# Low parts of an attention phase moved from GpSimd to VectorE, and three of fifteen prepared weight slabs parted later

## Chip, cores and metric

One core of one Trainium2 chip runs the whole program. The metric is the device time of one execution in microseconds (us); the median of several runs counts.

## What is computed

Two transformer blocks follow each other, on 1024 tokens of width 1024, in float32. The first has a convolution and retention mixer and an MLP; the second has sparse attention (DSA, 8 heads that share one key), latent attention (MLA, 8 heads), a gated merge and an MLP. The change touches the projection and the attention of the second block, and a preparation that runs inside the first. The reference of the second block, shortened:

```python
h = rmsnorm(x, attn_norm_g)
z = h @ w_in          # a_q, a_k, a_v, i_q, i_k, i_w, c_q, c_kv, k_r, g
y_a = dsa_sparse_attention(a_q, a_k, a_v, i_q, i_k, i_w, positions, rel_bias)   # top 256 keys of a query
q_nope, q_rope = split(rmsnorm(c_q) @ w_uq)
k_nope, v_b = split(rmsnorm(c_kv) @ w_ukv)
y_b = mla_attention(q_nope, rope(q_rope), k_nope, rope(k_r), v_b)
gates = sigmoid(g + b_gate)
x = x + (gates[0] * (y_a @ w_branch_a) + gates[1] * (y_b @ w_branch_b)) @ w_out
```

## The kernel before

**Products.** Each float32 product is three TensorE products of rounded parts: high by high, high by low, low by high (`mm3`, line 528). A high part (`wh` for weights, halves of `u` or `t` for data) is a rounding copy, on ScalarE; a low part (`wl`, and others) is the difference of the number and its high part, a subtraction. `unit` (line 534) is the product of a 1024 x 128 piece of a weight with 512 tokens: 24 matmuls of 128x512. In it the background work gets a tick four times, once for every six matmuls (`Background`, line 195).

**Weights.** `Stream` (line 344) brings the weights in the order of use: the sync engine (SP) loads 512 KB into a ring of three (`wr`), ScalarE makes the high part, and the engine in `lo_engine` makes the low one. An entry made by `parted` needs none of this: GpSimd's DMA queue fetches both parts, ready, from the scratch `slabd` in DRAM.

**Preparation.** `part_slabs` (line 2017) fills `slabd` during the first block, 15 slabs in two halves each, in two lanes of the background. A lane loads half a slab into one of two `t4` buffers by SP, yields for some ticks, then queues the high part on ScalarE, the low part on VectorE and the write to `slabd` on GpSimd's DMA queue, each by a tick of its own. ScalarE takes its instructions in order, so the one of the slab stands ahead of all that is queued behind it, whether its load has landed or not.

**Projection of the second block.** `z_phase` (line 2323) multiplies `h` by all columns of `w_in`. The bit search for the top 256 keys (`topk` lane) runs beside it on VectorE and ScalarE. Its last ten units, for the columns AK (key and value of DSA) and AQ to AQ+3P (queries of DSA), come as five weights for the first 512 tokens and the same five again for the second, each fetched twice from `slabd`. Two halves of `w_uq` and then `w_ukv`, which follow in the stream, are split as usual.

**Attention.** `attention` (line 2425) writes its order by a planner, `Plan` (line 273). Each `step` has an engine, a cost, a rank and needs; the planner keeps a clock of its own for each engine and takes the step that starts first, so the costs fix the order in which instructions stand on each engine. Heads 0 to 7 are MLA, 8 to 15 DSA. A head has a front (logits into PSUM, row maximum and biases on VectorE, exponentials on ScalarE) and a back (transposes, products with values). The low parts are steps of "Pool", which is GpSimd: of the rope rows of the key (`mla_begin`, line 2670) and of the queries (`rope_rows`, 2780), of the DSA queries and key (`dsa_inputs`, 2833, `dsa_begin`, 2861), of the attention outputs (`y_done`, 2603, `yb_part`, 2918) and of the first three branch weights (`branch_weights`, 2467); so are the additions that end `q_rope` (2689). GpSimd also issues most of attention's DMAs.

Of the kernel before, what the change touches and what calls it, by code (L numbers as in the profile page):

```python
# [11 lines left out]
F32 = mybir.dt.float32  # L12
# [7 lines left out]
P = 128  # L20
# [468 lines left out]
class Model:  # L489
# [922 lines left out]
    def plan_mlp(self, w1, w2):  # L1412
# [3 lines left out]
        for q in range(16):  # L1416
            c = 2 * q * P
            s.add(D, [(lambda raw: raw.rearrange("p (k m) -> p k m", k=8), w1[:, :, c:c + P])])
        for q in self.QUADS:
            self.plan_quad(w1[:, :, 2 * q * P:2 * q * P + P], w1[:, :, 2 * q * P + P:2 * q * P + 2 * P])  # L1420
        x = {"t": [None, None], "b": [None, None]}
# [65 lines left out]

    def plan_quad(self, wa, wb):

# [478 lines left out]
    def plan2(self):  # L1968
# [19 lines left out]
        lat, rest = [CQ, CQ + P, CKV], [AK, AQ, AQ + P, AQ + 2 * P, AQ + 3 * P]  # L1988
        self.slabs = gates[:2] + lat + gates[2:] + rest
        for cs in (gates[:2], lat, lat, gates[2:], rest, rest):  # L1990
            for c in cs:
                s.parted(self.slabd[:, self.slabs.index(c)], D)
        self.slabs = [w[:, c:c + P].rearrange("(k p) m -> p k m", p=P) for c in self.slabs]
        wq = a["w_uq_2"]
# [22 lines left out]
    def part_slabs(self, e):  # L2017
# [4 lines left out]
        for i, h in halves[e::2]:  # L2022
# [5 lines left out]
            nc.sync.dma_start(raw.rearrange("p (k m) -> p k m", k=4), self.slabs[i][:, 4 * h:4 * h + 4])  # L2028
            yield 2
            yield (raw,)  # L2030
# [292 lines left out]
    def z_phase(self, hs, f, acc, G2):  # L2323
# [65 lines left out]
        for m in range(NZ - 3, 16):  # L2389
# [5 lines left out]
            if m == NZ - 2:  # L2395
                latent_products()
        for H in range(2):
            for kind, m in (("akv", 0), ("aq", 0), ("aq", 1), ("aq", 2), ("aq", 3)):
                w = ws.next()
                p = self.ps()  # L2400
                self.unit(p, w, hs[H])
                self.z_evac(kind, m, H, p)
        bg.flush()
# [21 lines left out]
    def attention(self):  # L2425
# [32 lines left out]
        ws = self.ws  # L2458
        ws.lo_engine = self.nc.gpsimd
        self.branch_weights(starts[15])  # L2460
# [6 lines left out]
    def branch_weights(self, t):  # L2467

        ws, step = self.ws, self.plan.step
        for i in range(3):  # L2470
            a = step("ACT", 0.95, t + i, lambda i=i: ws.split_ahead(ws.used + i + 1), [self.room])
            step("Pool", 2.4, t + i, lambda i=i: ws.parts[ws.used + i][2](), [a])

# [129 lines left out]
    def y_done(self, t, n, x):  # L2603
# [13 lines left out]
        def low(engine):  # L2617
            engine.tensor_sub(self.ya[1][:, s], x["ys"], self.ya[0][:, s].bitcast(F32))
        a = step("ACT", 0.95, t, high, needs + [self.room])
        if n < 15:  # L2620
            step("Pool", 2.4, t, lambda: low(nc.gpsimd), [a], frees=("t4",))
        else:
            step("DVE", 1.2, t, lambda: low(nc.vector), [a], frees=("t4",))
# [46 lines left out]
    def mla_begin(self):  # L2670
# [10 lines left out]
        for i in range(3):  # L2681
            kh, kl = self.slot(i)[2:4]
            a = self.plan.step("ACT", 0.95, -20 + i, lambda kh=kh: nc.scalar.activation(kh[64:96], kr, AF.Copy))
            self.kr_steps.append(self.plan.step(
                "Pool", 2.4, -20 + i, lambda kh=kh, kl=kl: nc.gpsimd.tensor_sub(kl[64:96], kr, kh[64:96].bitcast(F32)),
                [a]))
        self.qr_steps = {g: [self.q_rope(g, H) for H in range(2)] for g in range(2)}

    def q_rope(self, g, H):
# [19 lines left out]
        def main():  # L2709
# [6 lines left out]
        b = step("DVE", 0.61, rank, main, [b], frees=("ps",))  # L2716
        return step("Pool", 1.3, rank, lambda: nc.gpsimd.tensor_add(dst[:, c], dst[:, c], x["t"]), [a, b],
                    frees=("t2",))
# [61 lines left out]
    def rope_rows(self, t, h, done):  # L2780
# [11 lines left out]
        def low():  # L2792
            qh, ql = self.slot(h)[0:2]
            nc.gpsimd.tensor_sub(ql[64:96], x["raw"][64:96], qh[64:96].bitcast(F32))
# [3 lines left out]
        return step("Pool", 2.4, t + 2, low, [b], frees=("t4",))  # L2798

# [33 lines left out]
    def dsa_inputs(self, h):  # L2833
# [13 lines left out]
        def low():  # L2847
            nc.gpsimd.tensor_sub(self.aqs[64:128, s], x["raw"][0:64], self.aqs[0:64, s].bitcast(F32))

# [11 lines left out]
    def dsa_begin(self):  # L2861
# [56 lines left out]
    def yb_part(self, t, m, H):  # L2918
# [239 lines left out]
    def run(self):  # L3158
# [44 lines left out]
```

## Time and profile before

| | us |
|---|---|
| median of 3 runs (lowest, highest) | 2674.82 (2673.29, 2676.94) |
| the profiled execution, its own time | 2677.41 |
| its span, first to last instruction | 2675.6 |
| TensorE busy | 2588.6 (97%) |
| VectorE busy | 1895.2 (71%) |
| ScalarE busy | 1334.5 (50%) |
| GpSimd busy | 366.4 (14%) |

The profile names engines PE (TensorE), DVE (VectorE), ACT (ScalarE), POOL (GpSimd) and SP (the sync engine, which only issues DMAs). A row's operation is written as output<-inputs with the tiles' names: `ps` and `pd` are PSUM, the others SBUF. All operations go through one helper and so stand at one line, L183; they are told apart by tiles and shapes. "[17.77 <-DMA t<-in_w_in]" says that the engine stood idle for 17.77 us before the instruction, and that what ended the wait was a DMA. Block 1 ends shortly after 1200 us of the span, the second block's projection (the z phase) then runs to about 1506 us and attention from there to about 1850 us.

### The profile page before, as it was taken

Reading aid. Unit: us, or ns where it says so; the run is one execution under the profiler, and the core shown is the slowest. Engines: PE = TensorE matmul, PEld = TensorE weight load, DVE = VectorE, ACT = ScalarE, POOL = GpSimd, SP = SyncE. Lnnn points to the kernel's source line nnn. Section 1 sums busy time; section 2 is a strip of 40 time slices with the busy share of each in tenths; the row PEclk is TensorE's granted clock in tenths of the full one; section 3 lists DMA queues with packets and bytes.
Section 4 is the critical chain, followed back from the end, with each engine's and each line's share of the span. In section 5 each row is a group of like instructions: output and inputs, shape, how many; then the busy total and the mean of one; then the engine's idle time right before and its main releaser. Section 6 shows DMA issues by size and latency. Waiting matters only on the chain.

```text
span 2675.6 us, 33677 instructions
## 1 busy us (share of the span) xinstructions
PE 2588.6 (97%) x12052; PEld 2079.3 (78%) x12052; DVE 1895.2 (71%) x3239; ACT 1334.5 (50%) x2208; POOL 366.4 (14%) x393
## 2 busy tenths in 40 slices
PE   4999999999999999999999999999999999999998
PEld 4777777777888878777878778777887888887886
DVE  6684576887665466877889878887557566646668
ACT  4562114565444343445676477885135554443334
POOL 5141111100000021000211411420000000002111
PEclk8999999999999999999999999999999999999999
DMA  6536638655445597645545501444455564459784
GB/s 207 186 106 217 192 116 272 220 185 152 147 138 197 188 268 212 190 116 170 138 150 169 185 15 40 145 149 136 149 171 160 185 224 142 154 186 268 189 252 146
DMA packets 371735, 456.98 MB, mean 171 GB/s; under 512 B 34014, under 2 KB 262285, under 8 KB 371053
## 3 DMA queue, kind: packets, MB, share of 16 engines
q1 hardware_dynamic: 332096, 311.07, 37.2%
q0 software_dynamic: 39136, 143.60, 18.8%
q8 instruction: 95, 1.56, 0.2%
q14 instruction: 76, 0.61, 0.1%
q10 hardware_dynamic: 332, 0.14, 0.0%
HBM read 361.70 MB, written 96.18 MB: 171 GB/s over the span
## 4 chain that ended last, share of the span: by engine, by line
PE 73%; DVE 10%; issue 6%; DMA 5%; ACT 4%; POOL 1%; SPq 0%; POOLq 0%; ACTq 0%; DVEq 0%
PE ps L183 50%; PE pd L183 22%; DVE u L183 4%; DVE t L183 3%; ACT u L183 2%; DMA t<-in_w_in 2%; ACT t L183 1%; DVE wl L183 1%; DVE tiny L183 1%; POOL u L183 1%; DMA slabd<-t 1%; DVE topk L183 1%; DMA u<-opd 1%; ACT wh L183 1%; DMA t<-aqd 0%
## 5 line engine op out<-in xcount | busy, mean ns | idle before, releaser
L183 PE MATMUL ps<-u,wh 128*128 128x512 f32 x3696 | 1173.3, 398 | 6.7 <-ACT u L183 4.2
L183 PEld LDWEIGHTS ps<-u,wh 128*128 128x128 f32 x3696 | 690.0, 188 | 177.0 <-ACT u L183 5.7
L183 PE MATMUL ps<-u,wl 128*128 128x512 f32 x1848 | 731.9, 396 | 0.6 <-DVE wl L183 0.6
L183 PE MATMUL pd<-u,wh 128*128 128x512 f32 x1472 | 480.3, 407 | 2.5 <-ACT u L183 1.6
L183 PEld LDWEIGHTS ps<-u,wl 128*128 128x128 f32 x1848 | 347.5, 188 | 86.4 <-DVE wl L183 1.3
L183 DVE TENSOR_TENSOR wl<-wr,wh 128x1024 fp32r<-128x1024 f32 (+3 forms) x213 | 229.9, 1080 | 162.5 <-ACT wh L183 156.0
L183 PEld LDWEIGHTS pd<-u,wh 128*128 128x128 f32 x1472 | 274.1, 190 | 70.9 <-issue 5.7
L183 PE MATMUL pd<-u,wl 128*128 128x512 f32 x736 | 292.4, 397 | 0.0
L183 ACT ACTIVATE wh<-wr 128x1024 fp32r<-128x1024 f32 (+3 forms) x225 | 207.2, 921 | 168.3 <-PE pd L183 78.9
L183 ACT ACTIVATE t<-ps 128x512 f32<-128x512 f32 (+7 forms) x347 | 176.6, 523 | 177.0 <-PE ps L183 164.1
L183 DVE TENSOR_TENSOR t<-ps,t 128x384 fp32r<-128x384 f32 (+3 forms) x354 | 192.5, 563 | 90.6 <-PE ps L183 59.7
L183 ACT ACTIVATE t<-t 128x512 f32<-128x512 f32 (+2 forms) x261 | 162.8, 626 | 168.9 <-DVE t L183 90.5
L183 DVE TENSOR_TENSOR u<-u 128x1024 fp32r<-128x1024 f32 (+3 forms) x154 | 154.1, 1002 | 68.1 <-ACT u L183 62.6
L183 ACT ACTIVATE u<-t 128x512 fp32r<-128x512 f32 (+4 forms) x158 | 127.5, 815 | 136.7 <-DVE t L183 110.8
L183 ACT ACTIVATE wh<-u 128x1024 fp32r<-128x1024 f32 x96 | 101.3, 1055 | 182.8 <-PE ps L183 116.8
L183 DVE TENSOR_TENSOR wl<-u,wh 128x1024 fp32r<-128x1024 f32 x96 | 117.3, 1222 | 88.0 <-ACT wh L183 87.9
L183 PE MATMUL ps<-wh,u 128*128 128x512 f32 (+1 forms) x576 | 173.7, 383 | 0.6 <-DVE u L183 0.6
L183 POOL DMA_DIRECT2D u<-opd x64 | 55.2, 1027 | 862.8 <-DMA u<-opd 758.2
L183 PEld LDWEIGHTS pd<-u,wl 128*128 128x128 f32 x736 | 139.2, 189 | 34.0
L183 PE MATMUL pd<-wh,u 128*128 128x512 f32 x512 | 162.0, 396 | 0.0
L183 ACT ACTIVATE u<-u 128x1024 fp32r<-128x1024 f32 (+8 forms) x111 | 97.6, 889 | 126.1 <-issue 57.1
L183 ACT ACTIVATE u<-ps 128x512 f32<-128x512 f32 (+2 forms) x171 | 95.9, 575 | 115.2 <-PE ps L183 109.2
(191 smaller groups left out, 3507.6 us busy)
## 6 DMA issues: line engine op xcount, KB each, us to landing
wr<-in_w_fc SPq DMA_DIRECT2D x64, 512.0 KB, 4.5
opd<-t SPq DMA_DIRECT2D x128, 256.0 KB, 3.7
u<-opd POOLq DMA_DIRECT2D x64, 512.0 KB, 10.5
wr<-in_w_ff SPq DMA_DIRECT2D x64, 512.0 KB, 4.5
wr<-in_w_in SPq DMA_DIRECT2D x60, 512.0 KB, 3.9
t<-opd SPq DMA_DIRECT2D x48, 512.0 KB, 4.8
u<-in_w_ada POOLq DMA_DIRECT2D x32, 512.0 KB, 4.7
wr<-in_w_out SPq DMA_DIRECT2D x32, 512.0 KB, 3.9
```

What stands on the lines that cost most here:

```text
L183: return fn(*args, **kw)
```

## The change

1. `slabd` has 12 slabs instead of 15. AK, AQ and AQ+P are no longer prepared in block 1; their entries in block 2 are loaded and split as usual. AQ+2P and AQ+3P still come from `slabd`.
2. The last ten units of the z phase become five weights, each used at once for both halves of the tokens, into a pair of PSUM banks. There are as many matmuls as before.
3. A preparation lane yields 4 ticks instead of 2 between a slab's load and its high part on ScalarE.
4. Low parts of the weights fetched after that point, among them the two of `w_uq`, are made by VectorE instead of GpSimd.
5. In attention all steps of "Pool" become steps of "DVE", at lower costs, and the planner writes its order anew. GpSimd is left with DMA issues.
6. `plan_quad` counts its alternating half slots from the first of its entries, which keeps the alternation as it was.

```diff
@@ plan_mlp, plan_quad
+        first = len(s.entries)
-            self.plan_quad(w1[...], w1[...])
+            self.plan_quad(first, w1[...], w1[...])
...
+        n -= first_n
         s.entry(first, load, after, half=n % 2)
@@ plan2
-        self.slabs = gates[:2] + lat + gates[2:] + rest
-        for cs in (gates[:2], lat, lat, gates[2:], rest, rest):
+        self.slabs = gates[:2] + lat + gates[2:] + rest[3:]
+        for cs in (gates[:2], lat, lat, gates[2:]):
             for c in cs:
                 s.parted(self.slabd[:, self.slabs.index(c)], D)
+        for c in rest:
+            if c in self.slabs:
+                s.parted(self.slabd[:, self.slabs.index(c)], D)
+            else:
+                s.cols(w, c)
@@ part_slabs
-            yield 2
+            yield 4
@@ z_phase
-        for H in range(2):
-            for kind, m in (("akv", 0), ("aq", 0), ("aq", 1), ("aq", 2), ("aq", 3)):
-                w = ws.next()
-                p = self.ps()
-                self.unit(p, w, hs[H])
-                self.z_evac(kind, m, H, p)
+        ws.lo_engine = nc.vector
+        for kind, m in (("akv", 0), ("aq", 0), ("aq", 1), ("aq", 2), ("aq", 3)):
+            w = ws.next()
+            p = self.pd()
+            self.unit(p[:, 0], w, hs[0])
+            self.unit(p[:, 1], w, hs[1])
+            for H in range(2):
+                self.z_evac(kind, m, H, p[:, H])
@@ attention
-        ws.lo_engine = self.nc.gpsimd
@@ branch_weights; the same edit in y_done, mla_begin, rope_rows, dsa_inputs, dsa_begin
-            step("Pool", 2.4, t + i, lambda i=i: ws.parts[ws.used + i][2](), [a])
+            step("DVE", 1.14, t + i, lambda i=i: ws.parts[ws.used + i][2](), [a])
@@ q_rope; the same edit in yb_part
-        return step("Pool", 1.3, rank, lambda: nc.gpsimd.tensor_add(dst[:, c], dst[:, c], x["t"]), [a, b],
+        return step("DVE", 0.6, rank, lambda: nc.vector.tensor_add(dst[:, c], dst[:, c], x["t"]), [a, b],
@@ run
-        self.slabd = self.dp.tile([P, 15, 2, D], F32, name="slabd")
+        self.slabd = self.dp.tile([P, 12, 2, D], F32, name="slabd")
```

**How the order moves, place one.** ScalarE in block 1, near 280 to 301 us of the trace. A row that reads `t_N<-t_N 128x512` is the high part of half a slab; `wh<-wr` is that of a weight which TensorE uses next. Before:

```order
L183 ACTIVATE t_3113<-ps 128x512
L183 ACTIVATE wh<-wr 128x1024
L183 ACTIVATE t_3071<-t_3071 128x512
L183 ACTIVATE t_3085<-t_3085 128x512
L183 ACTIVATE t_3178<-t_3178 128x512
L183 ACTIVATE wh<-wr 128x1024
L183 ACTIVATE t_3220<-t_3220 128x512
L183 ACTIVATE u<-ps 128x512
```

And in the changed kernel:

```order
L183 ACTIVATE t_3103<-ps 128x512
L183 ACTIVATE wh<-wr 128x1024
L183 ACTIVATE t_3086<-t_3086 128x512
L183 ACTIVATE t_3088<-t_3088 128x512
L183 ACTIVATE wh<-wr 128x1024
L183 ACTIVATE u<-ps 128x512
L183 ACTIVATE t_3312<-ps 128x512
L183 ACTIVATE t_3244<-t_3244 128x512
```

Every row `t_N<-t_N` here is half a slab. Before, three of them stood between the two `wh<-wr`; now two do, and the second `wh<-wr` and the `u<-ps` behind it stand ahead of the next two (t_3244 follows below, t_3246 after it).

**Place two.** VectorE at the start of attention, about 1505 us. The `wl<-wr,wh` is the low part of `w_ukv`; the rows with `ps,u` at 128x512 are the two multiplications of `q_rope`, in pairs. Before:

```order
L183 SCALAR_TENSOR_TENSOR u<-u,topk,t_12437 128x512
L183 TENSOR_TENSOR wl<-wr,wh 128x1024
L183 SCALAR_TENSOR_TENSOR t_12515<-ps,u 128x512
L183 SCALAR_TENSOR_TENSOR u<-ps,u 128x512
L183 SCALAR_TENSOR_TENSOR t_12534<-ps,u 128x512
L183 SCALAR_TENSOR_TENSOR u<-ps,u 128x512
L183 SCALAR_TENSOR_TENSOR u<-ps,u 64x512 x2
```

And in the changed kernel:

```order
L183 SCALAR_TENSOR_TENSOR u<-u,topk,t_12414 128x512
L183 TENSOR_TENSOR wl<-wr,wh 128x1024
L183 TENSOR_TENSOR u<-u 32x1024 x3
L183 SCALAR_TENSOR_TENSOR t_12483<-ps,u 128x512
L183 SCALAR_TENSOR_TENSOR u<-ps,u 128x512
L183 SCALAR_TENSOR_TENSOR t_12493<-ps,u 128x512
L183 TENSOR_TENSOR u<-u,t_12483 128x512
L183 SCALAR_TENSOR_TENSOR u<-ps,u 128x512
L183 SCALAR_TENSOR_TENSOR u<-ps,u 64x512
L183 TENSOR_TENSOR u<-u,t_12493 128x512
```

Three low parts of the key's rope rows now stand between `w_ukv` and the first multiplication of `q_rope`, and the two additions stand among the multiplications.

**Place three.** VectorE in head 9, in the changed kernel. Before, this stretch of VectorE held only rows that read PSUM, reciprocals and maxima; the low parts stood on GpSimd:

```order
L183 TENSOR_TENSOR t_14808<-ps,t_14808 64x256
L183 TENSOR_TENSOR t_14361<-ps,t_14808 64x256
L183 RECIPROCAL topk<-topk 128x1 x2
L183 TENSOR_TENSOR wl<-wr,wh 128x1024
L183 TENSOR_TENSOR u<-t_14784,u 64x1024
L183 TENSOR_TENSOR wl<-wr,wh 128x1024 x2
L183 TENSOR_TENSOR u<-t_14832,u 128x512
L183 TENSOR_TENSOR u<-t_14839,u 128x512
L183 TENSOR_TENSOR t_14885<-ps,t_14864 128x512
L183 TENSOR_TENSOR u<-t_14845,u 128x512
L183 TENSOR_TENSOR t_14897<-ps,t_14872 128x512
L183 ISA u,topk<-pd,u 128x896
L183 ISA topk 128x1
L183 TENSOR_TENSOR t_14915<-ps,t_14876 128x512
L183 TENSOR_TENSOR u<-t_14857,u 128x512
L183 TENSOR_TENSOR u<-t_14874,u 128x512
```

`wl<-wr,wh` are the low parts of three branch weights, `u<-t_14784,u 64x1024` that of a DSA query, and the 128x512 rows `u<-t,u` five of the eight low parts of MLA's output, whose data (`t`) GpSimd's queue loads from DRAM. All eight stand in this head.

## Rows read from the trace of the kernel before

**Rows 1.** Timeline, ScalarE, 280 to 301: start, length, operation, [idle before <- releaser].

```profile
280.08 1.16 ACT L183 ACTIVATE t<-t 128x512 fp32r<-128x512 f32 x2
299.01 0.63 ACT L183 ACTIVATE t<-t 128x512 fp32r<-128x512 f32 x1 [17.77 <-DMA t<-in_w_in]
299.55 1.04 ACT L183 ACTIVATE wh<-wr 128x1024 fp32r<-128x1024 f32 x1
```

**Rows 2.** Timeline, the sync engine's queue, around 292.

```profile
292.65 4.26 SPq L183 DMA_DIRECT2D t<-in_w_in  x2
```

**Rows 3.** Timeline, TensorE, around 304.

```profile
303.95 1.11 PE L183 MATMUL ps<-ident,t 128*128 128x128 f32 x4 [3.52 <-DVE t L183]
```

**Rows 4.** Stretch: busy PE, PEld, DVE, ACT, POOL (instructions); clock; DMA share, GB/s.

```profile
304.00:308.00 4.00, 4.00 (x12) 3.21 (x13) 3.46 (x8) 0.00 (x0) 2.18 (x3) 0.59 0.80 237
```

**Rows 5.** Stretch of the z tail, columns as in rows 4.

```profile
1436.00:1506.00 70.00, 70.00 (x302) 56.23 (x301) 66.81 (x155) 29.33 (x54) 15.04 (x20) 1.00 0.66 199
```

**Rows 6.** Timeline, VectorE, the end of the top-k.

```profile
1495.08 2.71 DVE L183 TENSOR_SCALAR t<-u,topk 128x640 f32<-128x640 f32 x1
...
1499.35 0.89 DVE L183 SCALAR_TENSOR_TENSOR t<-t,topk,t 128x640 f32<-128x640 f32 x1
1500.27 2.91 DVE L183 SCALAR_TENSOR_TENSOR u<-u,topk,t 128x640 bf16<-128x640 f32 x1
1503.10 0.47 DVE L183 TENSOR_SCALAR t<-u,topk 128x512 f32<-128x512 f32 x1
...
1506.33 1.22 DVE L183 TENSOR_TENSOR wl<-wr,wh 128x1024 fp32r<-128x1024 f32 x1
1507.47 0.69 DVE L183 SCALAR_TENSOR_TENSOR t<-ps,u 128x512 f32<-128x512 f32 x1
```

**Rows 7.** Groups of GpSimd, 1490 to 1505: busy us, mean ns.

```profile
L183 POOL TENSOR_TENSOR wl<-wr,wh 128x1024 fp32r<-128x1024 f32 x2 | 5.5, 2747 | 8.8 <-ACT wh L183 8.8
```

**Rows 8.** Timeline, GpSimd, the start of attention.

```profile
1506.77 7.77 POOL L183 TENSOR_TENSOR u<-u 32x1024 fp32r<-32x1024 f32 x3 [4.27 <-issue]
1514.61 2.52 POOL L183 TENSOR_TENSOR u<-u,t 128x512 f32<-128x512 f32 x2
...
1523.68 4.76 POOL L183 TENSOR_TENSOR u<-t,u 32x1024 fp32r<-32x1024 f32 x2 [5.10 <-ACT u L183]
```

**Rows 9.** Timeline, TensorE, the first front of attention.

```profile
1526.14 1.02 PE L183 MATMUL pd<-u 96*128 96x512 f32 x4 [0.50 <-POOL u L183]
```

**Rows 10.** Stretches at the start of attention.

```profile
1503.00:1527.00 24.00, 23.48 (x124) 19.31 (x124) 17.85 (x30) 15.41 (x24) 14.66 (x9) 1.00 0.62 223
1527.00:1560.00 33.00, 29.18 (x169) 24.10 (x169) 23.42 (x47) 22.67 (x48) 10.06 (x8) 0.90 0.11 34
```

**Rows 11.** Groups of GpSimd's arithmetic in attention.

```profile
L183 POOL TENSOR_TENSOR u<-t,u 64x1024 fp32r<-64x1024 f32 (+3 forms) x28 | 57.7, 2065 | 188.6 <-ACT u L183 187.2 <-issue 0.8 <-DVE t L183 0.5
L183 POOL TENSOR_TENSOR u<-u 32x1024 fp32r<-32x1024 f32 x3 | 7.8, 2613 | 4.3 <-issue 4.3
L183 POOL TENSOR_TENSOR wl<-wr,wh 128x1024 fp32r<-128x1024 f32 x3 | 7.2, 2394 | 0.1
L183 POOL TENSOR_TENSOR u<-u,t 128x512 f32<-128x512 f32 x4 | 5.0, 1271 | 0.1
```

**Rows 12.** Groups of VectorE in attention, by shape.

```profile
L183 DVE TENSOR_TENSOR t<-ps,t 128x512 fp32r<-128x512 f32 x96 | 64.3, 684 | 11.4 <-ACT t L183 8.7 <-POOL u L183 2.1
...
L183 DVE TENSOR_TENSOR u<-t,u 128x1024 fp32r<-128x1024 f32 x1 | 1.2, 1226 | 1.1 <-ACT u L183 1.1
```

**Rows 13.** Stretches of attention: heads 0 to 6, 7 to 12, 13 and 14.

```profile
1526.10:1675.70 149.60, 138.43 (x934) 118.06 (x935) 117.30 (x252) 111.03 (x240) 30.04 (x23) 0.97 0.11 35
1675.70:1784.70 109.00, 102.72 (x743) 84.52 (x742) 91.21 (x246) 91.94 (x204) 44.28 (x34) 1.00 0.50 150
1784.70:1818.20 33.50, 33.00 (x244) 27.03 (x242) 29.88 (x85) 26.55 (x63) 2.40 (x1) 1.00 0.47 143
```

**Rows 14.** Stretch: head 9 alone.

```profile
1712.30:1733.70 21.40, 18.13 (x130) 14.46 (x127) 15.50 (x45) 18.82 (x41) 14.18 (x13) 1.00 0.77 240
```

More of the change, by code (lines that the diff above doesn't have):

```diff
@@ L1418, in plan_mlp @@
             s.add(D, [(lambda raw: raw.rearrange("p (k m) -> p k m", k=8), w1[:, :, c:c + P])])
+        first = len(s.entries)
         for q in self.QUADS:
-            self.plan_quad(w1[:, :, 2 * q * P:2 * q * P + P], w1[:, :, 2 * q * P + P:2 * q * P + 2 * P])
+            self.plan_quad(first, w1[:, :, 2 * q * P:2 * q * P + P], w1[:, :, 2 * q * P + P:2 * q * P + 2 * P])
         x = {"t": [None, None], "b": [None, None]}
@@ L1486, in plan_mlp, with plan_quad @@
             s.entry(lambda hi, lo, d=d: parts(kept("t", d))(hi, lo))
-    def plan_quad(self, wa, wb):
+    def plan_quad(self, first_n, wa, wb):
         nc, s = self.nc, self.ws
@@ L2620, in y_done @@
         if n < 15:
-            step("Pool", 2.4, t, lambda: low(nc.gpsimd), [a], frees=("t4",))
+            step("DVE", 1.14, t, lambda: low(nc.vector), [a], frees=("t4",))
         else:
@@ L2684, in mla_begin @@
             self.kr_steps.append(self.plan.step(
-                "Pool", 2.4, -20 + i, lambda kh=kh, kl=kl: nc.gpsimd.tensor_sub(kl[64:96], kr, kh[64:96].bitcast(F32)),
+                "DVE", 1.14, -20 + i, lambda kh=kh, kl=kl: nc.vector.tensor_sub(kl[64:96], kr, kh[64:96].bitcast(F32)),
                 [a]))
@@ L2793, in low @@
             qh, ql = self.slot(h)[0:2]
-            nc.gpsimd.tensor_sub(ql[64:96], x["raw"][64:96], qh[64:96].bitcast(F32))
+            nc.vector.tensor_sub(ql[64:96], x["raw"][64:96], qh[64:96].bitcast(F32))
         a = self.transfer(2.6, t, load, self.qr_steps[h // 4] + done, takes=("t4",))
         b = step("ACT", 0.95, t + 2, high, [a])
-        return step("Pool", 2.4, t + 2, low, [b], frees=("t4",))
+        return step("DVE", 1.14, t + 2, low, [b], frees=("t4",))
     def latent_values(self, t, pair, c, done):
@@ L2847, in low @@
         def low():
-            nc.gpsimd.tensor_sub(self.aqs[64:128, s], x["raw"][0:64], self.aqs[0:64, s].bitcast(F32))
+            nc.vector.tensor_sub(self.aqs[64:128, s], x["raw"][0:64], self.aqs[0:64, s].bitcast(F32))
         t = starts[8 + h] - (20 if h < 2 else 12)
@@ L2853, in dsa_inputs @@
         b = step("ACT", 0.95, t + 3, high, [a])
-        c = step("Pool", 2.4, t + 3, low, [b], frees=("t4",))
+        c = step("DVE", 1.14, t + 3, low, [b], frees=("t4",))
         self.inputs[8 + h] = [c] + self.key_steps
@@ L2880, in low @@
         def low():
-            nc.gpsimd.tensor_sub(self.ak[0:64, D:2 * D], x["raw"][0:64], self.ak[0:64, 0:D].bitcast(F32))
+            nc.vector.tensor_sub(self.ak[0:64, D:2 * D], x["raw"][0:64], self.ak[0:64, 0:D].bitcast(F32))
         def low_again():
@@ L2904, in dsa_begin @@
         b = [step("ACT", 0.95, t + 3, lambda i=i: high(i), [a]) for i in range(2)]
-        c = step("Pool", 2.4, t + 3, low, [b[0]])
+        c = step("DVE", 1.14, t + 3, low, [b[0]])
         c = step("ACT", 0.95, t + 5, low_again, [c])
@@ L2930, in low @@
         def low():
-            nc.gpsimd.tensor_sub(self.yb[1][:, s], x["r"], self.yb[0][:, s].bitcast(F32))
+            nc.vector.tensor_sub(self.yb[1][:, s], x["r"], self.yb[0][:, s].bitcast(F32))
         a = self.transfer(3.2, t, load, [self.room, self.yd_steps[m]], takes=("t2",))
         b = step("ACT", 0.52, t, high, [a])
-        step("Pool", 1.3, t, low, [b], frees=("t2",))
+        step("DVE", 0.6, t, low, [b], frees=("t2",))
     def bias_next(self, h, qb):
```

## Prediction, made before the changed kernel ran

> **What bounds the kernel now.** TensorE is busy for 97% of the span (the page's first part, in the table above), so a part of the change matters only where TensorE stands idle or would begin to. I read in this order: the stretch of each place that the change touches, then the timeline of the engine that ends the waits there, then the groups, for durations. The reader is to see four things.
>
> In block 1 there is one clear stall: ScalarE waits 17.77 us, until 298.91, with the high part of a half slab [rows 1], whose load was issued only at 292.65 [rows 2]. The weight's high part behind it then comes at 299.55, and TensorE has nothing for 3.52 us up to 303.95 [rows 3]. After that the granted clock is 0.59 over 4 us [rows 4], which is 2.4 GHz falling to 1.2 GHz for part of the stretch, although TensorE is busy throughout.
>
> In the z tail TensorE is busy 70.00 of 70 us, and VectorE is nearly full as well: 66.81 [rows 5]. VectorE has 3 us to spare there.
>
> At the start of attention GpSimd is a chain of its own: three low parts from 1506.77, two additions until 1517.1, and, after a transfer, the low part from 1523.68 that lets the first front go [rows 8, 9]. Yet TensorE is busy 23.48 of the 24 us from 1503 to 1527 [rows 10], with products of the projections that the order puts there.
>
> In the heads, VectorE is busy 78% of heads 0 to 6 (117.30 of 149.60 us), 84% of heads 7 to 12 (91.21 of 109.00) and 89% of heads 13 and 14 (29.88 of 33.50); TensorE has 93, 94 and 99% [rows 13]. GpSimd is idle for most of it. This is the place where the change costs something: it moves all of GpSimd's arithmetic of attention to an engine that is four fifths full.
>
> **Block 1.** Six half slabs fewer mean six rounding copies of about 0.63 us on ScalarE [rows 1] and as many subtractions and transfers. ScalarE had waited 17.77 us in one piece, so that work is hidden and worth nothing in itself. The wait is what counts. In the changed order only two half slabs stand between the weights there instead of three (place one above), so the weight's high part no longer stands behind the one whose load was late. I take off 3.5 us of idle time [rows 3] and, for the clock, 0.41 x 4 = 1.6 us [rows 4], and round the two up to -6 for the smaller preparation waits later, whose loads get two ticks more: a tick is six matmuls. Below: -9, if those waits go too. Above: +2, if another half slab is late in its turn and stops ScalarE for less than before.
>
> **z tail.** Five weights used once instead of twice leave TensorE the same matmuls. Added are the loads of three weights, three high parts of 1.04 us [rows 1] and three low parts. Two of these (AK, AQ) were queued before the engine is switched and stay on GpSimd, one comes to VectorE, and so do the two of `w_uq`: 3 x 1.14 = 3.4 us more on VectorE, 1.14 being the distance of two starts, 1506.33 and 1507.47 [rows 6]. Against that stand the two GpSimd low parts that go (5.5 us, [rows 7]). Beside them two steps of the top-k took long: 2.71 us for one whose 512-wide like takes 0.47, and 2.91 for one whose 640-wide neighbour takes 0.89 [rows 6], some 4.2 us together. I expect the two new GpSimd low parts to hold up the count earlier by 0 to 4.8 us (two of 2.4, [rows 11]) and the high parts by 0 to 3. The top-k ends 3 us later by my reckoning (bounds -1 and +7).
>
> [...]
>
> **Start of attention.** VectorE now makes the three low parts of the key (place two above), 3 x 1.14 = 3.4 us, before the first multiplication of `q_rope`, which stood at 1507.47 [rows 6]. That moves to about 1507.5 + 3 + 3.4 = 1514. Four PSUM buffers let TensorE run on for some products, so it stalls about 5 us (1 to 9). The chain that GpSimd had is shorter: 7.77, 2.52 and 2.38 (half of 4.76) [rows 8] become 3.4, 1.2 and 1.14, which takes 6.9 us off. The later start gives back 3 plus the 1.14 of `w_ukv` and part of the multiplications between, so the first front comes at 1525 instead of 1526.14 [rows 9]. But the products that TensorE could not do before the front remain as filler for the 3.8 us that it idles from 1527 to 1560 [rows 10]. Net +0.5, between -4 and +6. With the z tail that is all: TensorE's own z work is not moved.
>
> **The low parts in the heads.** GpSimd loses 20 wide and 8 narrow subtractions (57.7 us), the three of the key, three weights and four additions [rows 11]: 77.7 us. On VectorE a wide one takes 1.226 us [rows 12] at a distance of 1.14, a 128x512 one about 0.69 at 0.61: 26 x 1.14 + 12 x 0.61 = 37 us. Most low parts end long before use, so a shorter one gains nothing by itself. What counts is where the 37 us stand.
>
> Heads 0 to 6: with 8 to 10 us more, VectorE comes to some 127 of 149.6 us, 85%. It has been above that in other stretches with TensorE at 99% [rows 13]. I take 0, between -6 (the planner spreads VectorE's work more evenly and some of TensorE's 11.2 idle us go) and +5.
>
> Heads 7 to 12: by the changed order all three weights stand here, seven of DSA's queries, two outputs and the eight narrow ones, so 12 wide and 8 narrow: 13.7 + 4.9 = 18.6 us. 91.21 + 18.6 = 109.8 us in a stretch of 109.00. This does not fit. At 95%, the most that VectorE reached in any stretch [rows 5], it needs 115.6; at the 89% of heads 13 and 14 [rows 13], 123. Against this: records of dense instructions overlap by the difference of 1.22 and 1.14, so the 109.8 holds some 3 us that are counted twice; and head 9, where TensorE idles 3.3 of 21.4 us and VectorE has 5.9 free [rows 14], takes the eight narrow ones. I take 95%, because all that matters was denser in the z tail than ever in attention: +6.6, rounded to +7, between -2 and +14. In heads 13 and 14 one more low part fits.
>
> **Sum.** -6 + 0.5 + 0 + 7 = +1.5 on the profiled 2677.41, so 2678.9. That execution is 2.6 us above the median of the runs shown, which gives 2676.3; I say 2677. A measurement of this kernel can tell about 0.2%, which is 5.3 us: the forecast is no change.
>
> **Rivals.**
> *VectorE takes it all.* The in-order engine keeps up, since the work in heads 7 to 12 can lag behind TensorE by the depth of its buffers and be made good in heads 13 to 15. Then the heads give 0 to -2, block 1 -6 and the start -1: 2677.41 - 2.6 - 8 = 2667. For it speaks head 9, where VectorE was held by GpSimd and not full; against it the 109.8 of 109.00.
> *VectorE becomes the bound.* Heads 8 and 9 hold the densest piece (place three above). The point from which it decides is a share of VectorE above some 92% over heads 7 to 12: then TensorE waits for VectorE in each head, at 91% the stretch is 109.8 / 0.91 = 120.7, +12, and the narrow low parts, in order behind transfers, hold up what follows. 2674.8 - 6 + 0.5 + 12 + 3 = 2684, slower. The Trainium skill ("Perfetto Trace Analysis", section "Optimizing Scalar/DVE Operations") says that with a saturated VectorE some work may be moved to ScalarE or even GpSimd; this change goes the other way. The trace bears it out for heads 7 to 12 alone.
> *The start stalls.* Three low parts on VectorE before `q_rope` cost TensorE 9 us, with a fall of the clock like that of [rows 4] behind it (1.6 us), and nothing of it comes back: 2676.3 + 9 = 2685.
> *The preparation does not do what it says.* Another half slab is late and ScalarE is stopped as long: block 1 gives 0 and the time is 2682. The order speaks against it at the one place, not at all others.
>
> **Chances and range.** My forecast 0.38; VectorE keeps up 0.28; VectorE as the bound 0.22; the start 0.06; the preparation 0.06. The middle case alone spans 2670 to 2680. The range of 2666 to 2689 takes in the other two large ones with a few us of the bounds beyond them. Faster by over 0.2% is the second case, 0.28; slower is the last three, 0.34.
>
> **What would show it.** Block 1: no idle time of TensorE over 2 us near 300, and the clock at 1.0 after it. Start: the first multiplication of `q_rope` near 1514 less the 6 us of block 1, and a TensorE wait for VectorE of about 5 us there. Heads 7 to 12: VectorE at 93 to 96%, the stretch near 116 us, most of the added idle time of TensorE put down to VectorE in heads 8 to 10. I am wrong if that stretch is no longer than before with VectorE near 97%, or if heads 0 to 6 change by over 5 us.

## The result and the profile after

The changed kernel takes 2698.15 us (median of 4 runs, 2697.16 to 2700.24) against 2675.88 us before (4 runs, 2673.29 to 2680.07). The ratio is 1.0082, with a 95% interval of 1.0069 to 1.0094: 22 us slower. The profiled execution took 2697.36 us with a span of 2695.6 us. So the forecast of no change was wrong, and the time lies 9 us above the range.

The busy times of the page:

```profile
PE 2595.7 (96%) x12052; PEld 2086.0 (77%) x12052; DVE 1929.5 (72%) x3274; ACT 1333.9 (49%) x2205; POOL 275.4 (10%) x333
```

TensorE has 7 us more than before for the same number of matmuls (12052); its mean granted clock is 0.986 for 0.989. VectorE has 34 us more, GpSimd 91 less.

**Block 1 and the z tail went much as forecast.** Stretches of the changed kernel around 300 us, then of the z tail (busy time of PE, PEld, DVE, ACT, POOL; clock; DMA), to hold against [rows 4, 5]:

```profile
297.00:301.00 4.00, 4.00 (x21) 3.15 (x20) 1.75 (x4) 0.00 (x0) 0.00 (x0) 1.00 0.98 321
301.00:305.00 4.00, 4.00 (x16) 2.68 (x15) 0.00 (x0) 1.43 (x3) 0.00 (x0) 1.00 0.04 12
1431.00:1501.00 70.00, 70.00 (x302) 56.23 (x301) 64.50 (x157) 31.78 (x57) 4.55 (x5) 1.00 0.37 111
```

TensorE works through at 2.4 GHz where it stood for 3.5 us before. Counting matmuls off in both traces, the changed kernel is 5.2 us further ahead behind this place than ahead of it, and 2 us more by 560 us. It loses 3 us between 900 and 1200 us. Of these, 1.1 are a longer wait for VectorE at 1149 us (3.1 us for 2.0), and (1 - 0.57) x 4 = 1.7 are a fall of the clock at 1099 us, behind waits of 1.8 and 0.95 us. The kernel before has waits of 1.6 and 0.95 us at the same point of its work, at 1107 us, and no fall; why is not shown. The changed kernel, then the kernel before:

```profile
1099.00:1103.00 4.00, 3.97 (x10) 3.16 (x11) 3.97 (x5) 1.57 (x2) 0.00 (x0) 0.57 0.42 108
```

```profile
1107.00:1111.00 4.00, 3.99 (x17) 3.27 (x18) 3.97 (x5) 1.56 (x2) 0.00 (x0) 1.00 0.44 104
```

The top-k's last scan then starts only 2.7 us earlier than before (1500.90 for 1503.61).

**The stall at the start of attention was as forecast too.** VectorE, TensorE:

```profile
1502.16 0.75 DVE L183 SCALAR_TENSOR_TENSOR t<-t,topk,t 128x512 f32<-128x512 f32 x1
...
1504.87 3.49 DVE L183 TENSOR_TENSOR u<-u 32x1024 fp32r<-32x1024 f32 x3
1508.38 0.69 DVE L183 SCALAR_TENSOR_TENSOR t<-ps,u 128x512 f32<-128x512 f32 x1
1509.13 1.22 PE L183 MATMUL ps<-u,wh 128*128 128x512 f32 x2 [4.99 <-DVE t L183]
```

The three low parts of the key take 3.49 us ahead of `q_rope`, and TensorE waits 4.99 us for VectorE (5 were forecast). The first front begins at 1522.55 us instead of 1525.01; [rows 9] shows the third product of the latter, which waited for GpSimd. The first products of the front, in the kernel before and in the changed one:

```profile
1525.01 0.63 PE L183 MATMUL pd<-u 96*128 96x512 f32 x2
```

```profile
1522.55 1.38 PE L183 MATMUL pd<-u 96*128 96x512 f32 x6
```

**The heads did not.** The same stretches as in [rows 13] (heads 0 to 6, 7 to 12, 13 and 14), and head 9 alone, [rows 14]:

```profile
1522.60:1680.30 157.70, 142.76 (x943) 120.75 (x942) 133.17 (x271) 112.11 (x243) 6.23 (x12) 0.97 0.09 29
1680.30:1808.90 128.60, 113.61 (x769) 92.13 (x767) 111.21 (x268) 94.96 (x205) 7.95 (x15) 0.95 0.44 129
1808.90:1842.30 33.40, 32.83 (x241) 27.10 (x240) 30.68 (x86) 26.22 (x62) 0.00 (x0) 1.00 0.50 143
1721.30:1752.00 30.70, 24.21 (x155) 19.56 (x154) 27.24 (x62) 24.07 (x49) 5.37 (x10) 0.89 0.58 180
```

The stretch of heads 0 to 6 in [rows 13] begins behind the start of the first front. From that start on, the kernel before has

```profile
1525.00:1675.70 150.70, 139.07 (x937) 118.25 (x936) 118.40 (x254) 112.11 (x241) 31.14 (x24) 0.97 0.11 37
```

So heads 0 to 6 take 157.7 us for 150.7, and heads 7 to 12 take 128.6 for 109.0, of which head 9 has 9.3. Part of this is not lost: TensorE does more of its work there (3.7 us more of busy time in heads 0 to 6 at the same clock, 769 records for 743 in heads 7 to 12), and from head 13 to the end the program is 4.2 us shorter. So -2.4 up to the first front, +7.0, +19.6, -4.2: the 20 us between the two spans. VectorE's busy time in heads 7 to 12 is 111.21 us; 109.8 were forecast. But its share is 86%, not 95%, and the clock is 0.95 instead of 1.00. In head 9, TensorE's waits:

```profile
1727.53 0.39 PE L183 MATMUL ps<-t,u 128*128 128x256 f32 x1 [1.87 <-ACT t L183]
1731.93 0.90 PE L183 MATMUL ps<-t,u 128*64 128x256 f32 x3 [4.02 <-DVE t L183]
```

It stands for 1.87 and 4.02 us, while VectorE and ScalarE go through the low parts of place three.

### The profile page after: what moved, and what is told of

The parts are those of the page before. It is cut to its first block, busy times and chain, and to the rows that moved or that the text cites. A ratio compares the mean times of both kernels' runs of the same rounds, so it can differ in the third digit from the quotient of the medians.

```text
span 2695.6 us, 33590 instructions
## 1 busy us (share of the span) xinstructions
PE 2595.7 (96%) x12052; PEld 2086.0 (77%) x12052; DVE 1929.5 (72%) x3274; ACT 1333.9 (49%) x2205; POOL 275.4 (10%) x333
## 4 chain that ended last, share of the span: by engine, by line
PE 77%; DVE 9%; issue 5%; ACT 5%; DMA 2%; SPq 0%; POOL 0%; ACTq 0%; DVEq 0%; POOLq 0%
PE ps L183 52%; PE pd L183 25%; DVE u L183 4%; ACT u L183 3%; DVE t L183 2%; ACT t L183 1%; DVE tiny L183 1%; DVE topk L183 1%; DVE wl L183 1%; DMA t<-in_w_in 1%; DMA u<-opd 1%; ACT wh L183 1%; DMA t<-opd 0%; DMA u<-in_w_ada 0%; DMA t<-u 0%
## 5 line engine op out<-in xcount | busy, mean ns | idle before, releaser
L183 PE MATMUL ps<-u,wh 128*128 128x512 f32 x3536 | 1122.3, 398 | 13.2 <-DVE t L183 5.0
L183 PEld LDWEIGHTS ps<-u,wh 128*128 128x128 f32 x3536 | 659.7, 188 | 175.2 <-ACT u L183 5.7
L183 PE MATMUL ps<-u,wl 128*128 128x512 f32 x1768 | 700.4, 396 | 0.6 <-DVE wl L183 0.6
L183 PE MATMUL pd<-u,wh 128*128 128x512 f32 x1632 | 531.0, 406 | 2.7 <-ACT u L183 1.8
L183 PEld LDWEIGHTS ps<-u,wl 128*128 128x128 f32 x1768 | 332.4, 188 | 83.0 <-DVE wl L183 1.3
L183 PEld LDWEIGHTS pd<-u,wh 128*128 128x128 f32 x1632 | 304.6, 190 | 78.6 <-issue 5.8
L183 PE MATMUL pd<-u,wl 128*128 128x512 f32 x816 | 324.0, 397 | 0.0
L183 ACT ACTIVATE t<-ps 64x256 f32<-64x256 f32 (+7 forms) x337 | 170.1, 521 | 163.3 <-PE ps L183 159.6
L183 DVE TENSOR_TENSOR u<-u 128x1024 fp32r<-128x1024 f32 (+4 forms) x157 | 157.6, 1006 | 68.4 <-ACT u L183 63.6
L183 DVE TENSOR_TENSOR u<-t,u 128x512 fp32r<-128x512 f32 (+4 forms) x157 | 144.0, 922 | 32.0 <-ACT u L183 30.7
```

What stands on the lines that cost most here:

```text
L183: return fn(*args, **kw)
```

## The experiments

Two theories at first. **Load**: VectorE's 37 us more hold TensorE up. **Order**: the planner, with other costs, writes an order in which TensorE waits, whichever engine makes the low parts. "On GpSimd" means planned with GpSimd's costs and run there. Median before, on the same chips, was 2675.9 to 2676.5 us throughout. A table stands at the end of this section.

**All low parts back, and the changed order with GpSimd.** In e1 all the steps of attention are as before; in e2 the planner's costs stay those of the change, and only the engine that runs the step differs:

```diff
-        c = step("DVE", 1.14, t + 3, low, [b], frees=("t4",))     # e1; so all seven kinds
+        c = step("Pool", 2.4, t + 3, low, [b], frees=("t4",))
-            nc.vector.tensor_sub(self.aqs[64:128, s], x["raw"][0:64], ...)    # e1 and e2
+            nc.gpsimd.tensor_sub(self.aqs[64:128, s], x["raw"][0:64], ...)
```

e1 was expected to do this:

> All of attention's low parts and additions are planned for and run on GpSimd again; slabs, z tail and preparation stay changed. In the trace of the changed kernel attention (from the last product of the z phase to the merge) is 26 us longer and all before it is about 6 us shorter. Load theory (VectorE, with 37 us more, holds TensorE up) and order theory (the planner writes a worse order, because its costs let VectorE look emptier than it is) both say that attention returns to what it was: 2675.9 - 6 = 2670 us, between 2667 and 2673. If it stays above 2680, the z tail or the slabs have made attention longer.

e2 was expected to do this:

> Planned as in the changed kernel (low parts at VectorE's costs), so that every engine but GpSimd keeps the changed kernel's order, but the low parts and additions run on GpSimd. Load theory: VectorE loses 37 us of work, TensorE no longer waits; 2670 us, between 2666 and 2676. Order theory: the order of fronts, backs and transfers is what costs, so 2690 to 2700 us, as in the changed kernel.

e1 took 2681.2 us (ratio 1.0017, 1.0006 to 1.0028), e2 2701.0 (1.0082, 1.0069 to 1.0095). So the loss is in attention, and the changed order is slow without VectorE's work too. In heads 0 to 6 of e2 no engine waits for a low part of GpSimd, and they take 156.7 us (147.5 in e1). Its heads 7 to 12 prove less, since GpSimd's low parts are late in head 9: VectorE waits 15.36 us for them, and TensorE 11.71 us behind it.

```profile
1524.50:1681.20 156.70, 144.12 (x937) 122.15 (x935) 120.03 (x256) 110.51 (x238) 29.53 (x23) 0.95 0.09 26
```

```profile
1738.10 0.69 DVE L183 TENSOR_TENSOR t<-ps,t 128x512 fp32r<-128x512 f32 x1 [15.36 <-POOL u L183]
1738.84 0.90 PE L183 MATMUL ps<-t,u 128*64 128x256 f32 x3 [11.71 <-DVE t L183]
```

e1 was 11 us above its expectation. Its start shows why, GpSimd and VectorE:

```profile
1501.14 8.06 POOL L183 TENSOR_TENSOR u<-u 32x1024 fp32r<-32x1024 f32 x3 [34.47 <-ACT u L183]
1501.54 2.71 DVE L183 SCALAR_TENSOR_TENSOR t<-t,topk,t 128x512 f32<-128x512 f32 x1
1504.29 2.71 DVE L183 SCALAR_TENSOR_TENSOR u<-u,topk,t 128x512 bf16<-128x512 f32 x1
1506.92 3.35 DVE L183 TENSOR_TENSOR wl<-wr,wh 128x1024 fp32r<-128x1024 f32 x1
PE ps L183 <- DVE t L183: 7.4, 1, 7.4
```

With the low parts of `w_uq` on VectorE, GpSimd is free at 1501 us and makes the key's low parts beside the end of the top-k. Two of VectorE's steps take 2.71 us each, where the first takes 0.75 in the changed kernel (above), and the low part of `w_ukv` takes 3.35 for 1.22 [rows 6]. TensorE waits 7.4 us, the last of these rows. This is the contention that the Trainium skill states ("SBUF — State Buffer", section "Who interferes with whom": two SBUF inputs on VectorE against a GpSimd instruction that reads SBUF); here the trace agrees.

**Which low parts.** e3 puts back all but the key's rope rows, MLA's rope rows and the additions; e4 puts back only the three weights and the eight narrow ones; both edits are of the kind of e1:

```diff
-            step("DVE", 1.14, t + i, lambda i=i: ws.parts[ws.used + i][2](), [a])      # weights, in e3 and e4
+            step("Pool", 2.4, t + i, lambda i=i: ws.parts[ws.used + i][2](), [a])
-        step("DVE", 0.6, t, low, [b], frees=("t2",))                                   # narrow ones, in e3 and e4
+        step("Pool", 1.3, t, low, [b], frees=("t2",))
```

e3 was expected to do this:

> Low parts of DSA's queries and key, of the outputs and of the branch weights back on GpSimd (20 wide less 8 of MLA's rope rows, 3 weights, 8 narrow); the key's rope rows, MLA's rope rows and the additions of q_rope stay on VectorE, some 15 of the 37 us. Load theory, cost in proportion: 26 x 15 / 37 = 10 us over e1, 2680. Theory of the crowded place (what costs are the 11 low parts in a row in head 9 and DSA's queries just ahead): heads 7 to 12 return to 109 us, 2672 to 2675 us.

e4 was expected to do this:

> Only the three branch weights and the eight 128x512 low parts, which all stand in head 9, are back on GpSimd (8.3 of the 37 us). Load theory: 26 x 8.3 / 37 = 6 us less than the changed kernel, 2692. Theory of the crowded place: head 9 (30.7 us in the changed kernel) falls to 18 to 20 us, and the time to 2684 to 2688.

e3: 2680.4 us (1.0014, 1.0005 to 1.0022) which is the load theory's number, but by luck: that theory has 10 us over e1, and e3 is 0.8 below e1. e4: 2696.9 (1.0067, 1.0054 to 1.0080), 5 us above that theory. The crowded place in head 9 is not the cause: without it the kernel is 1 us faster. Head 9 falls from 30.7 us to 23.8, and most of that is lost again in the heads behind it.

**The start alone, and the old order with VectorE.** e5 is e1 with the key's rope rows and the additions on VectorE. e6 is the converse of e2: planned at GpSimd's costs, run on VectorE.

```diff
-            nc.gpsimd.tensor_sub(self.aqs[64:128, s], x["raw"][0:64], ...)     # e6 from e1; so all seven kinds
+            nc.vector.tensor_sub(self.aqs[64:128, s], x["raw"][0:64], ...)
-                "Pool", 2.4, -20 + i, lambda kh=kh, kl=kl: nc.gpsimd.tensor_sub(kl[64:96], ...),     # e5 from e1
+                "DVE", 1.14, -20 + i, lambda kh=kh, kl=kl: nc.vector.tensor_sub(kl[64:96], ...),
```

e5 was expected to do this:

> Like e1, but the key's three low parts and the four additions of q_rope stay on VectorE; TensorE's order is e1's but for 14 rows. In e1's trace the three low parts run on GpSimd from 1501 to 1509 us, just when VectorE ends the top-k, and its steps take 2.71 us for 0.75; TensorE then waits 7.4 us. Theory of contention at the start: the first front comes 21.7 us after the last scan of the top-k, as in the changed kernel, instead of 27.7, and the heads keep e1's 305 us: 6 us less than e1, so 2669 to 2676 us and faster than before by 0 to 7. If the order of the heads is as sensitive as in e3, they take 308 to 315 us and the gain is gone.

e6 was expected to do this:

> The converse of e2: planned with GpSimd's costs, so TensorE's and ScalarE's order are e1's row by row, but all the low parts and additions run on VectorE, where the plan's sequence puts them. Load theory: VectorE has the same 37 us more as in the changed kernel, so 2690 to 2700 us. Order theory: 2670 to 2680 us, because the old order holds, and the start gains the 6 us of e5.

e5: 2678.8 us (1.0006, 0.9997 to 1.0015), 3 us above the range of the contention theory: the heads take 310 us, not 305, which is the case of the expectation's last sentence. e6: 2701.4 (1.0092, 1.0076 to 1.0107). So in the old order VectorE's work costs 22.6 us over e5. Each theory alone is refuted by the other's run: order by e6, load by e2 and by e8, which follows. The two costs do not add.

**DSA's queries and key.** e7 is e5 with these nine on VectorE; e8 is e4's order with rope rows, queries, key and outputs run on GpSimd.

```diff
-        c = step("Pool", 2.4, t + 3, low, [b], frees=("t4",))                   # e7 from e5
+        c = step("DVE", 1.14, t + 3, low, [b], frees=("t4",))
-            nc.vector.tensor_sub(ql[64:96], x["raw"][64:96], ...)               # e8 from e4; the step stays "DVE"
+            nc.gpsimd.tensor_sub(ql[64:96], x["raw"][64:96], ...)
```

e7 was expected to do this:

> Like e5, with the nine low parts of DSA's queries and key on VectorE too (planned and run there); MLA's rope rows, outputs and branch weights on GpSimd. e4 showed that heads 6 to 15 stay slow without the weights and narrow low parts; if the queries are the cause, heads 8 to 15 take 145 to 150 us (137 in e1) and the time is 2685 to 2692; if it is the rope rows with them, 2672 to 2680.

e8 was expected to do this:

> TensorE's order is e4's row by row (planned with all but weights and narrow low parts on VectorE), but rope rows, queries, key and outputs run on GpSimd; key's rope rows and additions on VectorE. It repeats e2 without the late GpSimd low parts in head 9. Order theory: 2690 to 2698 us, as e4. Load theory: VectorE loses 23 of its 29 us, so 2672 to 2680.

e7: 2695.6 us (1.0064, 1.0049 to 1.0080); e8: 2689.3 (1.0044, 1.0029 to 1.0060). Nine low parts, 10 us of VectorE, cost 17 us, more than was expected. e8 runs each low part on the same engine as e5 and differs in the order alone, which costs 10.5 us; e4, with e8's order and 23 us more on VectorE, is 7.6 us slower than e8. In the old order VectorE's work makes heads 0 to 6 long (e6), in the new order they are long without it (e8). Heads 0 to 6 of e5, e6 and e8, to hold against e2 above:

```profile
1525.10:1677.20 152.10, 140.18 (x950) 119.31 (x949) 122.73 (x259) 111.59 (x240) 27.36 (x21) 0.98 0.10 31
1527.90:1690.60 162.70, 145.53 (x936) 124.72 (x936) 129.79 (x264) 110.75 (x238) 5.74 (x11) 0.91 0.08 24
1520.90:1677.20 156.30, 143.03 (x937) 121.10 (x935) 122.09 (x258) 111.12 (x241) 27.70 (x21) 0.96 0.09 28
```

GpSimd's queue in e5 and in e7 shows what else is different. A query's load is `t<-aqd`; `yd<-t` writes out the output of a pair of heads, here first that of heads 4 and 5 and then that of heads 6 and 7. Both tiles come from the two `t4` buffers. First e5, then e7:

```profile
1674.99 0.57 POOL L183 DMA_DIRECT2D yd<-t  x1 [0.55 <-DVE t L183]
1675.56 0.54 POOL L183 DMA_DIRECT2D t<-aqd  x1
...
1699.14 0.54 POOL L183 DMA_DIRECT2D t<-aqd  x1 [0.29 <-POOL u L183]
...
1711.45 0.57 POOL L183 DMA_DIRECT2D yd<-t  x1 [3.93 <-DVE t L183]
```

```profile
1675.21 0.51 POOL L183 DMA_DIRECT2D t<-aqd  x1 [8.60 <-DVE u L183]
1676.70 0.57 POOL L183 DMA_DIRECT2D yd<-t  x1 [0.98 <-DVE t L183]
1679.91 0.52 POOL L183 DMA_DIRECT2D t<-aqd  x1 [2.65 <-DMA yd<-t]
...
1700.74 0.51 POOL L183 DMA_DIRECT2D t<-aqd  x1 [6.90 <-DVE u L183]
1720.06 0.57 POOL L183 DMA_DIRECT2D yd<-t  x1 [18.81 <-DVE topk L183]
```

In e7 one query's load comes ahead of the write of heads 4 and 5, and the next one waits 2.65 us for that write. The output of heads 6 and 7 leaves 8.6 us later. This gave a third theory. **Buffer**: the planner's greedy choice gives the second `t4` to a query's load instead of to the output tile of the next head pair, since at VectorE's lower cost a buffer comes free at another moment of the plan; the back of that pair starts late. In e8, where GpSimd makes these low parts, the queue has the late order as well (that output leaves at 1718.82), so it comes from the planned cost and not from the engine.

**The buffers' order by itself.** e10 and e11 add needs to the changed kernel and to e7; e12 forces the late order on e5.

```diff
+        if new:
+            self.begins = getattr(self, "begins", {})
+            self.begins[n] = first
...
-                 + [self.dsa_room], takes=("t4",))
+                 + [self.dsa_room] + ([self.begins[(0, 6, 6, 6, 8, 8, 10, 10)[h]]] if h else []), takes=("t4",))
@@ e12, in place of the last line
+                 + [self.dsa_room] + ([self.begins[{2: 6, 3: 6, 4: 6, 5: 8, 6: 8, 7: 10}[h]]] if h > 1 else []), takes=("t4",))
+        if h in (1, 4, 6):
+            y, i = self.begins[{1: 6, 4: 8, 6: 10}[h]], a.needs[0]
+            y.needs.append(i)
+            y.wait += 1
+            i.users.append(y)
```

e10 was expected to do this:

> The changed kernel, except that the planner may start the load of a DSA query only when the output tile of the head pair before it has taken its t4 buffer (queries 1 to 3 after heads 6 and 7, 4 and 5 after 8 and 9, 6 and 7 after 10 and 11), which is the order that the kernel before has. All low parts stay on VectorE. Theory of the buffer (a query's load takes the second t4 first, since VectorE's shorter low part frees it earlier, and the back of a head pair starts late): 5 to 8 us less than the changed kernel, and what is left is VectorE's work: 2690 to 2693. Load theory alone: 2698 as before.

e11 was expected to do this:

> e7 (only DSA's queries and key, the key's rope rows and the additions on VectorE), with that same order of the t4 buffers. Buffer theory: the 17 us that e7 lost against e5 come back, 2676 to 2682 us. Load theory (nine low parts on VectorE): 2695, as e7.

e12 was expected to do this:

> The converse, on e5: queries and key on GpSimd, VectorE's work as in e5, but the output tile of heads 6, 8 and 10 may take its t4 buffer only after one more query's load, as in e7 and the changed kernel. Buffer theory: heads 7, 9 to 11 grow as in e7, 2690 to 2697 us, with no work added to VectorE. Load theory: 2679, as e5.

e10: 2692.4 us (1.0055, 1.0039 to 1.0070), e11: 2684.5 (1.0024, 1.0014 to 1.0034), e12: 2688.6 (1.0040, 1.0025 to 1.0056). The order of the buffers gives back 11 us of e7's 17, costs 10 us in e5, where VectorE has nothing more to do, and is worth 6 us in the changed kernel. e10 lies in the range of its theory; e11 got back less than was expected, and e12 lost a little less. Heads 7 to 12 of e5, of e12 and of e10, with VectorE's busy time third:

```profile
1677.20:1786.80 109.60, 104.10 (x734) 85.86 (x742) 91.31 (x246) 91.95 (x203) 44.29 (x34) 0.98 0.52 149
```

```profile
1677.90:1799.60 121.70, 111.92 (x746) 91.43 (x756) 92.34 (x247) 93.73 (x204) 44.19 (x35) 0.94 0.46 138
```

```profile
1683.60:1805.50 121.90, 108.67 (x752) 87.22 (x760) 111.54 (x269) 93.50 (x205) 8.85 (x17) 1.00 0.45 138
```

e5 and e12 have 91 and 92 us of VectorE, and 109.6 against 121.7 us of time, two fifths of the difference by the clock (0.98 and 0.94: 5 us). e10 has the buffers' order of e5 and 20 us more of VectorE, and takes 121.9 us.

**Time or waiting.** A low part on VectorE waits until ScalarE has made the high part and holds back what is queued behind it. e13 gives VectorE the time without that wait: row maxima that nobody reads, beside the low parts on GpSimd.

```diff
+            nc.vector.reduce_max(self.idle[0:64], x["raw"][0:64], axis=mybir.AxisListType.X)
             nc.gpsimd.tensor_sub(self.aqs[64:128, s], x["raw"][0:64], ...)
```

e13 was expected to do this:

> e5, order unchanged on TensorE, and ahead of 28 of the low parts on GpSimd (rope rows, queries, key, outputs; not the weights) VectorE makes a row maximum of the same data, into a column that nobody reads: about the same time on VectorE as the low part (some 27 of the 33 us), with one SBUF operand, ready long before, so that VectorE does not wait for ScalarE there. Theory of VectorE's time: 2678.8 + 22 x 27 / 33 = 2697 us, near e6's 2701. Theory of the wait for ScalarE: below 2686 us.

2699.5 us (1.0080, 1.0064 to 1.0095): 20.7 us over e5 for 28 maxima of 29.5 us together (10.8, 9.7, 5.4 and 3.6 by their groups). So VectorE's time alone has this price, without the wait for ScalarE. One thing was not separated: a maximum also holds the `t4` tile that it reads, and one load waits 1.26 us for a maximum (the third row). Heads 0 to 6 and 7 to 12 of e13, and that load:

```profile
1529.20:1693.10 163.90, 144.66 (x948) 123.60 (x947) 133.71 (x268) 111.83 (x240) 27.27 (x21) 0.94 0.09 26
1693.10:1808.30 115.20, 105.84 (x733) 86.31 (x742) 103.87 (x262) 92.72 (x204) 44.20 (x34) 0.99 0.49 145
1655.07 0.57 POOL L183 DMA_DIRECT2D t<-akvd  x1 [1.26 <-DVE idle L183]
```

VectorE is at 82 and 90%, and TensorE waits for it in both: in heads 0 to 6 the largest wait is

```profile
PE ps L183 <- DVE t L183: 11.3, 8, 2.4
```

where e5 has 5.5 us in 9 pieces and the kernel before 3.8 in 6.

**The preparation.** e9 is the kernel before with one edit, e14 is e1 with one:

```diff
-            yield 2                             # e9, part_slabs
+            yield 4
-        ws.lo_engine = nc.vector                # e14, z_phase, ahead of the last five weights
```

e9 was expected to do this:

> The kernel before with one edit, four ticks instead of two between a slab's load and its high part; fifteen slabs, z tail and attention unchanged. The changed kernel is 5.2 us ahead at 324 us of its trace and 7 us by 560. If the place in ScalarE's queue does it, the same is seen here, the stall at 300 is gone, and nothing is lost after it: 2668 to 2672 us, faster than before by 4 to 8. If the three slabs fewer are needed for it, 2674 to 2677.

e14 was expected to do this:

> e1 without the one line that hands the low parts of the z tail's last weights to VectorE: slabs, waits and the five weights used once stay changed, attention is as before. GpSimd is then busy with the low parts of w_uq as before, and the key's rope rows come only when the top-k is over. Theory of contention at the start: the first front comes 21 to 23 us after the last scan of the top-k (27.7 in e1), so 4 to 6 us less than e1: 2674 to 2677 us, equal to the kernel before or a little faster. If not, e1's loss lies elsewhere: 2681.

e9: 2683.9 us (1.0032, 1.0023 to 1.0041), so slower, and not as expected. The stall at 300 is gone, but fifteen slabs with the longer waits last until 541 us, where the first block's MLP begins. ScalarE and TensorE of e9 there:

```profile
539.45 0.63 ACT L183 ACTIVATE t<-t 128x512 fp32r<-128x512 f32 x1 [7.91 <-DMA t<-in_w_in]
541.56 1.22 PE L183 MATMUL ps<-u,wh 128*128 128x512 f32 x2 [9.25 <-ACT u L183]
```

The last write to `slabd` is issued at 541.1 us there, at 494.6 in the changed kernel and at 517.7 before. So the three slabs fewer are what makes the longer wait harmless there. e14: 2676.7 us (0.9997, 0.9988 to 1.0006), 4.5 us less than e1, as the contention theory had it, and equal to the kernel before: without the fourth and the fifth part of the change, the rest gains nothing that these runs can tell. No version beats the kernel before clearly.

The extra work of VectorE in attention over e5 (low parts at their distances of 1.14 and 0.61 us; in e13 as measured) and the order of the buffers:

| run | us | VectorE's work over e5, us | order of the `t4` buffers |
|---|---|---|---|
| e5 | 2678.8 | 0 | old |
| e12 | 2688.6 | 0 | late |
| e8 | 2689.3 | 0 | late, planned for VectorE |
| e3 | 2680.4 | 9 | old |
| e11 | 2684.5 | 10 | old |
| e7 | 2695.6 | 10 | late |
| e4 | 2696.9 | 23 | late, planned for VectorE |
| e10 | 2692.4 | 31 | old, planned for VectorE |
| e13 | 2699.5 | 29.5 | old, planned for GpSimd |
| e6 | 2701.4 | 31 | old, planned for GpSimd |
| changed | 2698.2 | 31 | late, planned for VectorE |

## Why the prediction was wrong

- **Block 1, -6**: right in mechanism and place, too large in the end. TensorE gained 5.2 us there and 2 by 560 us; 3 us were lost again by 1200 us. e14, which has the change without its fourth and fifth parts, equals the kernel before (0.9988 to 1.0006, or -3.2 to +1.6 us), so at most some 3 us of the -6 are left. The part that I costed at nothing, three slabs fewer, is what the gain depends on (e9). One reading was off: ScalarE's wait ended at 299.01 [rows 1], not at 298.91; nothing is worked out from it.
- **z tail and start, +0.5**: the last scan of the top-k 3 us later against TensorE's own matmuls, and TensorE's wait of 5 us, as forecast. The front was not: the product of [rows 9] was to come at 1525 less the 6 of block 1, and came at 1523. I did not see that GpSimd's low parts of the key would collide with the top-k once VectorE makes those of `w_uq` (e1). The fourth part of the change brings that collision and the fifth avoids it; with neither (e14) it is not there. The rival of the start leaves the 1.6 us of its own fall of the clock out of its sum.
- **Heads 0 to 6, 0**: this step failed. They took 7.0 us longer, 3.3 of it idle time of TensorE. VectorE got 15 us more there, not 8 to 10 (133.17 for 118.40), and some 85% of the stretch was taken as harmless because other stretches ran at 89%. In the old order the work is not harmless (162.7 us in e6 and 163.9 in e13, for 152.1 in e5). In the new order these heads are as long with the low parts on GpSimd (156.7 in e2, 156.3 in e8) as on VectorE, so there the order is enough. What in it costs the time is not shown.
- **Heads 7 to 12, +7 (to +14)**: this step failed most; it measured +19.6. The load was right (111.2 for 109.8 us), the limit was not: I took 95% from the z tail, where TensorE does not wait at all [rows 5], and the kernel reached 86%. Below that limit I gave VectorE's time no price. The runs price it: in the old order 20.7 us for 29.5 (e13) and 22.6 for 31 (e6), some 0.7 us for each; in orders planned with it, 13.6 for 31 (e10), 5.7 for 10.3 (e11) and 1.6 for 9 (e3) over e5, 7.6 for 23 (e4 over e8) and 7.0 for 10.3 (e7 over e12), some 0.2 to 0.7. The idle fifth of VectorE is no free room. Before, it lay in pieces between the steps of a head (in heads 7 to 12, 11.3 us behind ScalarE in 21 pieces of at most 1.5), and work put there delays the next link of the chain from TensorE to VectorE, ScalarE and back. That last clause is argued from these rows; the price is shown. Beside VectorE's time stood a cost that I had not looked for: the planner's order of the two `t4` buffers, 6 us in the changed kernel (e10), 11 in e7. The order was there to be read; I read it for where the low parts stand and not for which tile takes a buffer first.
- **The clock**: (1 - 0.97) x 157.7 and (1 - 0.95) x 128.6 make 11 us lost to the lower level, against 4.5 before [rows 13]. Of the 26.6 us in heads 0 to 12, 6 to 7 are this. That it is a second price of the same waits is argued only: heads 7 to 12 of e10 have 13.2 us of idle time at a clock of 1.00. I had counted it for a rival alone.
- Of the rivals, "VectorE becomes the bound" came nearest in sign and place, at 0.22; it gave 2684 and missed the buffers. The rule named with it (the Trainium skill, "Perfetto Trace Analysis", section "Optimizing Scalar/DVE Operations") lets work be moved from a saturated VectorE even to GpSimd; in the old order that pays 22.6 us (e5 against e6), although VectorE without the work is only 81 and 83% busy (e5, heads 0 to 6 and 7 to 12).

## What to carry to other kernels

An engine that feeds another in short turns may have no free time to give away, however idle its average looks. Here work added to VectorE at some 80% cost about 0.7 us for each us where the order was made without it, and 0.2 to 0.7 where the planner knew of it: price it before counting it as free. Where a planner writes the order, a changed cost can change choices far from the edit; compare which step takes each scarce buffer first, and hold the old order by a need if it was better. Test a shift from one engine to another both ways: the new order on the old engine, and the old order on the new one.

## What was not expected

The two costs do not add: over e5, VectorE's work costs 22.6 us in the old order (e6), the new order costs 10.5 without that work (e8), and the changed kernel, with both, is 19.4 us slower. The late buffers cost 6 us beside VectorE's work (e10 to the changed kernel) and 10 without it (e5 to e12); the intervals do not tell these two apart. A longer wait in the preparation, alone, moved the stall from 300 us to 541 us and made it 9.25 us for 3.52.
